# Fifteen small loads queued behind the first early store of a row-sum kernel

## The chip, the core and the metric

The kernel runs on one core of one Trainium2 chip. The metric is device time in microseconds (us), the median of several runs. The kernel before takes 161.08 us (median of 3 runs, 160.9 to 161.12).

## What is computed

```python
# x: float32 [32, 512, 1024]
relu_x = np.maximum(x, 0)
return np.sum(relu_x, axis=-1).astype(np.float32)     # float32 [32, 512]
```

The input is seen as 16,384 rows of 1,024 numbers, 64 MiB in all. Each row is clamped at zero and summed; the output is one number a row, 64 KiB.

## The kernel before

**Tiling.** Each of the 128 partitions holds 128 rows, counted as columns 0 to 127 of the tile `res` [128, 128], in which the sums gather. Rows come in blocks of 16 for each partition (8 MiB for a block) into three rotating tiles, `io0` to `io2`. There are seven full blocks and a tail of 16 rows, which is loaded in smaller and smaller pieces: 8 rows, 4 rows, then 2,302, 873 and 518 numbers of the last four rows, and at last 403 numbers into a small tile of its own, `last`.

**Work on a block.** ScalarE clamps a block or half a block in place (`clamp`, L145) and VectorE sums it (`total`, L153). In the last blocks and the tail both engines take single rows, with clamp and sum in one instruction: ScalarE in `act_row` (L160), VectorE in `dve_row` (L168); the parts of the last rows are `act_part` (L122) and `dve_part` (L127). GpSimd clamps one small piece (L246). A few matrix multiplies (L186) run near the end, whose product nobody reads. The last but one sum is finished by VectorE at L266, which reads `last` and so waits for the last load; the last one is finished by ScalarE with `act_part` on the rest of `last`.

**The SP queue.** SP (SyncE) issues all DMAs, in the order in which they are written. It issues the loads of the seven blocks (`load`, L104), of which those from the fourth on wait for VectorE to be done with the tile that they overwrite; then the six loads of the tail, of which the first waits; then three stores (`store`, L111 to L119):

- the early store of the first 16 columns of `res`, whose sums were done long before,
- the middle store of the next 110 columns, behind a wait at L115 for ScalarE and one on the DMA itself (L116) for VectorE,
- the last store of 2 columns, which waits for `sems.end`, that is for L266 and the last `act_part`.

Then SP clears the other semaphores (L51) and waits at L52 until all stores have landed: each DMA adds 16 to the semaphore `stored`, and `n_store` counts the DMAs that do so. With that the program ends. The order on each engine is written out by hand; no scheduler moves instructions. The first load stands ahead of everything else in the program.

Of the kernel before, what the change touches and what calls it, by code (L numbers as in the profile page):

```python
# [4 lines left out]
F32 = mybir.dt.float32  # L5
# [21 lines left out]

EARLY = 1
N_MM, MM_COLS = 8, 512


def kernel(tc: tile.TileContext, x: bass.AP, out: bass.AP):
    nc = tc.nc
    sems = Semaphores(tc)

    tc.close()
    tc.compile()
    nc.cur_bb = nc.bb_map[tc.start_bb_name]
    body = nc.cur_bb.bb.instructions
    ends = list(body)  # L40
    body.clear()
    n_stores = relu_sum(nc, sems, x, out)
    body.extend(ends)


    nc.cur_bb = nc.bb_map[tc.start_bb_name + "_end"]
    nc.cur_bb.bb.instructions.clear()
    nums = sorted(s.num for s in (*sems.loads, sems.act, sems.dve))
    cleared = range(nums[0], nums[-1] + 1)
    assert len(cleared) == len(nums)  # L50
    nc.sync.sem_clear(cleared)  # L51
    nc.sync.wait_ge(sems.stored, 16 * n_stores).then_inc(sems.stored, -16 * n_stores)  # L52
    open_without_barrier(tc, EARLY)
# [12 lines left out]
def relu_sum(nc, sems: Semaphores, x: bass.AP, out: bass.AP):  # L66
    x_flat = x.flatten_outer_dims()
# [27 lines left out]
    def sums(m, n):  # L95
        if m < ROWS:
            return of[:, m : m + n], res[:, m : m + n]
        return ov[:, m - ROWS : m - ROWS + n], res[:, m : m + n]
# [12 lines left out]
    def store(m, n, act, sem, count):  # L111
        nonlocal n_store
        dst, src = sums(m, n)
        if act:
            nc.sync.wait_ge(sems.act, act)  # L115
        nc.sync.dma_start(out=dst, in_=src).wait_op(sem, count, "sem-ge").then_inc(  # L116
            sems.stored, 16
        )
        n_store += 1  # L119
# [100 lines left out]
    for n in TAIL:  # L220
# [26 lines left out]
        out=clamped, in0=clamped, scalar1=0.0, scalar2=None, op0=MAX  # L247
    ).wait_op(loaded, 16, "sem-ge").then_inc(sems.end, 1)
    for lo, hi, n, first, second in (
# [9 lines left out]


    store(0, ROWS, freed[0][0], sems.dve, freed[0][1])
    store(ROWS, NT - ROWS - 2, sums_act, sems.dve, sums_dve)


# [2 lines left out]
        out=clamped,  # L267
# [59 lines left out]
```

## Time and profile before

| | |
|---|---|
| Median of 3 runs | 161.08 us (160.9 to 161.12) |
| Profiled execution, from its first to its last instruction (span) | 159.9 us; the page has no other time of it |
| Median less span | 1.2 us, around the span |
| VectorE busy | 118.7 us (74%) |
| ScalarE busy | 103.6 us (65%) |
| TensorE busy | 8.6 us (5%) |
| DMA packets of the kernel | 2304, 67.18 MB, 97.8% of 16 engines' time |
| Mean DMA rate over the span | 420 GB/s |
| Sixteen DMA issues of SP | 13 loads, 3 stores |

The profile is one execution on the chip. Times inside it count from the start of its span. "SPq" is the SP engine's queue of DMA issues; "idle before, releaser" names what ended a wait. The page's DMA share is the mean busy share of the 16 DMA engines that carry out what SP issues; a DMA over 128 partitions shows as 128 packets of data and 16 of 4 bytes, which are the increments of its semaphore: 16 DMAs with 144 packets each make the 2304. The trace also keeps the start, duration and size of every packet (without the number of its DMA engine), and the time at which each increment of a semaphore landed.

### The profile page before, as it was taken

To read this page: it belongs to the slowest core of one execution; us is meant where nothing else is said; L and a number is where in the kernel's file an instruction comes from. 1 tells how busy PE (TensorE), PEld (TensorE's weight loads), DVE (VectorE), ACT (ScalarE), POOL (GpSimd) and SP (SyncE) were. 2 spreads that over 40 slices of the span, in tenths; PEclk is the share of its full clock that TensorE was granted. 3 is DMA by queue.
4 is the path that set the end of the run, shared out by engine and by line. 5 is a ranking of instruction groups with operands and counts; after the bars stand their busy time and mean duration, and the time that the engine had idled before them with its cause. 6 is when DMAs were issued, how large, how long until landed. Compare 5 with 4: busy or idle time off the path is not lost.

```text
span 159.9 us, 157 instructions
## 1 busy us (share of the span) xinstructions
PE 8.6 (5%) x16; PEld 3.6 (2%) x16; DVE 118.7 (74%) x44; ACT 103.6 (65%) x53; POOL 1.0 (1%) x5
## 2 busy tenths in 40 slices
PE   0000000000000000000000000000000000000695
PEld 0000000000000000000000000000000000000241
DVE  0000000006999799999999999999999799999986
ACT  0000049993599807997099950999429993397995
POOL 0000000000000000000000000000000000000001
DMA  8996996996996997999979979969969969899993
GB/s 279 508 492 295 524 492 295 524 492 295 525 492 295 524 475 311 524 393 393 525 328 459 508 344 459 508 295 508 492 295 524 492 295 524 377 402 402 428 396 110
DMA packets 2304, 67.18 MB, mean 420 GB/s; under 512 B 640, under 2 KB 768, under 8 KB 1024
## 3 DMA queue, kind: packets, MB, share of 16 engines
q1 hardware_dynamic: 2304, 67.18, 97.8%
HBM read 67.11 MB, written 0.07 MB: 420 GB/s over the span
## 4 chain that ended last, share of the span: by engine, by line
DMA 45%; DVE 45%; ACT 9%; SPq 1%; issue 0%
DMA io<-in_x_dram 45%; DVE res L153 43%; ACT io L145 9%; DVE io L168 1%; SPq L104 1%; DVE io L127 1%; DVE io L266 0%
## 5 line engine op out<-in xcount | busy, mean ns | idle before, releaser
L153 DVE TENSOR_REDUCE res<-io 128x8 f32<-128x8192 f32 (+2 forms) x10 | 101.1, 10173 | 39.2 <-ACT io L145 39.2
L145 ACT ACTIVATE io<-io 128x8192 f32<-128x8192 f32 (+2 forms) x10 | 81.8, 8218 | 25.9 <-DMA io<-in_x_dram 25.9
L160 ACT ACTIVATE io<-io 128x1024 f32<-128x1024 f32 x18 | 18.8, 1042 | 6.6 <-DMA io<-in_x_dram 6.6
L186 PE MATMUL ps<-io 128*128 128x512 f32 x16 | 8.6, 698 | 149.5 <-DVE io L168 149.5
L168 DVE TENSOR_SCALAR_CACHE_REDUCE io<-io 128x1024 f32<-128x1024 f32 x14 | 16.2, 1215 | 0.5 <-DMA io<-in_x_dram 0.4
L143 ACT ACT_TABLE_LOAD x1 | 1.3, 1283 | 22.3 <-DMA io<-in_x_dram 22.3
L186 PEld LDWEIGHTS ps<-io 128*128 128x128 f32 x16 | 3.6, 231 | 153.7 <-DVE io L168 149.5
L160 ACT ACTIVATION_READ_ACCUMULATOR io<-io 128x1 f32 x18 | 3.3, 186 | 0.0
L246 POOL TENSOR_SCALAR io<-io 128x254 f32<-128x254 f32 x1 | 0.8, 841 | 155.4 <-DMA io<-in_x_dram 155.4
L168 DVE DVE_READ_ACCUMULATOR io<-io 128x1 f32 x14 | 1.2, 82 | 0.0
L127 DVE TENSOR_SCALAR_CACHE_REDUCE io<-io 128x552 f32<-128x552 f32 (+1 forms) x2 | 1.1, 594 | 0.0
L122 ACT ACTIVATE io<-io 128x321 f32<-128x321 f32 (+1 forms) x2 | 0.9, 426 | 0.1
L266 DVE SCALAR_TENSOR_TENSOR io<-last,io 128x254 f32<-128x254 f32 x1 | 0.4, 423 | 0.0
L122 ACT ACTIVATION_READ_ACCUMULATOR io<-io 128x1 f32 x2 | 0.4, 186 | 0.0
L122 ACT ACTIVATE last<-last 128x153 f32<-128x153 f32 x1 | 0.3, 330 | 0.0
L122 ACT ACTIVATION_READ_ACCUMULATOR last<-last 128x1 f32 x1 | 0.2, 187 | 0.0
L127 DVE DVE_READ_ACCUMULATOR io<-io 128x1 f32 x2 | 0.2, 82 | 0.0
L311 POOL MEMSET const-uint8-127<- 128x1 uint8 x1 | 0.1, 102 | 0.0
L311 POOL MEMSET const-bfloat16-1.0<- 128x1 bf16 x1 | 0.1, 101 | 0.0
L311 POOL MEMSET const-float32-0.0<- 128x1 f32 x1 | 0.1, 99 | 0.2 <-issue 0.2
L311 POOL MEMSET const-float32-1.0<- 128x1 f32 x1 | 0.1, 98 | 0.0
L266 DVE DVE_READ_ACCUMULATOR io<-last,io 128x1 f32 x1 | 0.1, 82 | 0.0
## 6 DMA issues: line engine op xcount, KB each, us to landing
io<-in_x_dram SPq DMA_DIRECT2D x1, 4096.0 KB, 23.7
io<-in_x_dram SPq DMA_DIRECT2D x1, 2048.0 KB, 28.3
io<-in_x_dram SPq DMA_DIRECT2D x1, 1151.0 KB, 30.6
io<-in_x_dram SPq DMA_DIRECT2D x1, 436.5 KB, 31.2
io<-in_x_dram SPq DMA_DIRECT2D x1, 259.0 KB, 31.4
last<-in_x_dram SPq DMA_DIRECT2D x1, 201.5 KB, 31.4
io<-in_x_dram SPq DMA_DIRECT2D x7, 29.0
out_dram<-res SPq DMA_DIRECT2D x1, 55.0 KB, 1.6
```

Source lines behind the costliest of these rows:

```text
L104: dma = nc.sync.dma_start(out=dst, in_=src)
L122: nc.scalar.activation(out=ap, in_=ap, func=RELU, accum_out=accum_out).wait_op(*after, "sem-ge").then_inc(sems.end, 1)
L127: i = nc.vector.tensor_scalar(out=ap, in0=ap, scalar1=0.0, scalar2=None, op0=MAX, op1=ADD, accum_out=accum_out,)
L143: nc.scalar.preload_act_table(RELU).wait_op(loaded, 16, "sem-ge")
L145: i = nc.scalar.activation(out=ap, in_=ap, func=RELU)
L153: nc.vector.tensor_reduce(out=res[:, m : m + n], in_=ap, axis=mybir.AxisListType.X, op=ADD).wait_op(sems.act, n_act, "sem-ge").then_inc(se ...
L160: i = nc.scalar.activation(out=ap, in_=ap, func=RELU, accum_out=accum_out)
L168: i = nc.vector.tensor_scalar(out=ap, in0=ap, scalar1=0.0, scalar2=None, op0=MAX, op1=ADD, accum_out=accum_out,)
L186: i = nc.tensor.matmul(ps[:, :], rows_of[:, 0, :P], rows_of[:, 1, :MM_COLS], start=True, stop=True)
L246: nc.gpsimd.tensor_scalar(out=clamped, in0=clamped, scalar1=0.0, scalar2=None, op0=MAX).wait_op(loaded, 16, "sem-ge").then_inc(sems.end, 1)
L266: nc.vector.scalar_tensor_tensor(out=clamped, in0=last[:, : 2 + LAST_DVE], scalar=0.0, in1=clamped, op0=MAX, op1=ADD, accum_out=res[:, NT ...
L311: nc = _bacc.Bacc("TRN2", target_bir_lowering=False, num_devices=1)
```

## The change

Fifteen loads are put between the early store and the middle store. Load n, for n from 1 to 15, takes the first 20 + n numbers (84 to 140 bytes) of the first n rows of x, into a new tile `probe` of 16 partitions; no instruction reads that tile. The new loads wait for nothing, are issued from SP like the others, and add to `stored`, so that L52 waits for them too (18 DMAs instead of 3). No other instruction changes; from L29 on lines are numbered one higher, and eight higher from L262 on.

```diff
@@ -27,6 +27,7 @@
 
 EARLY = 1
 N_MM, MM_COLS = 8, 512
+PROBES, PROBE_COLS = 15, 64
 
 
 def tile_relu_sum_kernel(tc: tile.TileContext, x: bass.AP, out: bass.AP):
@@ -259,6 +260,13 @@
 
 
     store(0, ROWS, freed[0][0], sems.dve, freed[0][1])
+    probe = nc.alloc_sbuf_tensor("probe", [16, PROBES * PROBE_COLS], F32)
+    for n in range(1, PROBES + 1):
+        to = (n - 1) * PROBE_COLS
+        nc.sync.dma_start(
+            out=probe[:n, to : to + 20 + n], in_=x_flat[:n, : 20 + n]
+        ).then_inc(sems.stored, 16)
+        n_store += 1
     store(ROWS, NT - ROWS - 2, sums_act, sems.dve, sums_dve)
 
 
```

## The prediction

> **What bounds the kernel now.** I read the chain that ended last first, as shares and then its last pieces in order of time, since the change touches only the end of the DMA-issuing queue (SP).
>
> ```profile
> DMA io<-in_x_dram 45%; DVE res L153 43%; ACT io L145 9%; DVE io L168 1%; SPq L104 1%; DVE io L127 1%; DVE io L266 0%
> ```
>
> ```profile
> 125.15 30.57 DMA io<-in_x_dram
> 155.72 0.02 issue
> 155.75 1.23 DVE io L168 x2
> 156.97 1.05 DVE io L127 x4
> 158.03 0.02 issue
> 158.05 0.43 DVE io L266 x2
> ```
>
> The input stream (67 MB) sets the time almost to the end. From 125.15 us on the chain is the tail's loads; then short VectorE pieces, and L266, which needs two things: the DVE parts before it (done at 158.01) and the last load. The trace's landing records put the sixteen increments of that load at 157.10 to 158.03, fourteen of them by 157.56 and the other two at 157.91 and 158.03. So the tail is a tie of VectorE and the last load, and whatever delays that load delays the end one for one.
>
> Next the SP queue's timeline from 124 us on, and its waits:
>
> ```profile
> 124.29 2.31 SPq L104 DMA_DIRECT2D io<-in_x_dram  x5
> 126.65 0.44 SPq L104 DMA_DIRECT2D last<-in_x_dram  x1
> 127.21 31.63 SPq L116 DMA_DIRECT2D out_dram<-res  x3
> ```
>
> ```profile
> SPq L104 <- DVE res L153: 121.6, 5, 53.3
> SPq L115 <- ACT io L160: 29.3, 1, 29.3
> SPq L116 <- DVE io L266: 1.1, 1, 1.1
> SPq L52 <- SPq L52: 1.0, 1, 1.0
> ```
>
> Every load of the tail is issued by 127.1. The early store (rows 0 to 15) is issued at 127.21 and takes 0.38; then SP waits 29.3 us at L115, till 156.92, issues the middle store at 157.00, and the last store at 158.51. The DMA issues and the DMA share of the last microseconds:
>
> ```profile
> out_dram<-res SPq DMA_DIRECT2D x1, 55.0 KB, 1.6
> out_dram<-res SPq DMA_DIRECT2D x1, 8.0 KB, 31.0
> out_dram<-res SPq DMA_DIRECT2D x1, 1.0 KB, 1.4
> ```
>
> ```profile
> 156.00:157.00 1.00, 1.00 (x3) 0.38 (x2) 1.00 (x3) 1.00 (x3) 0.64 (x1) 1.00 0.95 333
> 157.00:158.00 1.00, 1.00 (x3) 0.19 (x1) 1.00 (x4) 0.90 (x4) 0.00 (x0) 1.00 0.22 60
> 158.00:159.00 1.00, 0.10 (x1) 0.00 (x0) 0.44 (x4) 0.43 (x3) 0.00 (x0) 1.00 0.09 23
> 159.00:160.00 1.00, 0.00 (x0) 0.00 (x0) 0.00 (x0) 0.00 (x0) 0.00 (x0) 1.00 0.08 1
> ```
>
> The early store took 31.0 us to land because each DMA engine works its queue in order: the packet records have none of its 64-byte packets before 156.55, after the last load's packets on that engine. So the fifteen new loads, queued behind it, run there too, after 156.5. And there (the last but one column) the DMA engines are busy 22%, 9% and 8% of the time.
>
> **The change part by part.** Nothing is removed. All is made against the profiled execution's 159.9 us; the median of the timed runs, 161.08, stands 1.2 above, and I carry that over.
>
> *SP's time.* Fifteen issues. The sixteen issues of this trace took 0.33 to 0.49 us each, so 5.0 to 7.3 us. SP reaches L115 at 132.6 to 134.9 instead of 127.6 and waits there 22 to 24 us instead of 29.3. Price 0. The new loads wait for no semaphore, and behind them are only the two stores and L52. The cover is gone when one issue costs over 29.3 / 15 = 1.95 us, four times the dearest row; beyond that each microsecond delays the middle store, and the last store once 1.5 more are used.
>
> *The loads ahead.* All thirteen loads of x are issued before the new ones, and engines take packets in order, so no packet of x goes later. Price 0; the bound upward is one engine's whole new work (next step).
>
> *DMA engines.* The new loads make 1 + 2 + ... + 15 = 120 rows of 84 to 140 bytes, 13 KB. A packet's time in the records: 1612 bytes 68 ns, 2072 bytes 85 ns, thus 0.037 ns a byte and 8.4 ns fixed; the small ends are 64 bytes 11 ns and 4 bytes (a completion) 9 ns. So a new packet is about 12 to 14 ns with 9 for its completion. If each partition goes to its own engine, the first engine gets fifteen: 15 x 22 = 0.33 us. If every row went to one engine: 120 x 13 + 15 x 9 = 1.7 us. On the latest engine the early store's packets end at 157.64, the middle store's fill 157.84 to 158.18, and the last store's start at 159.34. Idle there: 0.20 + 1.16 = 1.36 us; on most engines 0.5 to 0.9 more. 0.33 fits; 1.7 would stick out by 0.3 on the latest engine alone. I take 0.33, hence price 0: the middle store goes perhaps 0.13 later, and only L52 at 159.9 wants it.
>
> *Completions.* What the trace doesn't show is a row of fifteen tiny DMAs, each closing with a completion. The nearest row is the early store behind the last load: on the earliest engine they landed at 157.10 and 157.29, on the latest at 158.03 and 158.20, so 0.17 to 0.19 apart, though 0.065 of packets lay between. So one more DMA in an engine's queue costs from its packets, 0.02, to 0.17 or so if a completion must be acknowledged before the next DMA's data is written. 15 x 0.02 = 0.3, hidden as above; 15 x 0.17 = 2.6, not hidden (rival 1). I take the lower, because the 0.17 includes the early store's eight packets and a write to HBM, where the new loads write one packet to SBUF. Nothing in this makes the kernel faster: no wait is shortened, and below nothing I allow only the scatter of the runs.
>
> That fixed costs of DMAs overlap, the landings show: the last three loads landed at 156.85, 157.51 and 158.03, 0.66 and 0.52 apart, as their bytes need, while one store alone takes 1.4 us from issue to landing. The Trainium skill (DMA: Bandwidth & Descriptors, "Anatomy of one DMA") has about 2 us fixed for each DMA, most of it the write receipt, and calls the bubble of the semaphore write itself tiny. Paid one after another that would be an estimated 30 us here; by the landings just given the trace agrees with the tiny bubble and not with the sum.
>
> *The end.* L52 now waits for 18 landings instead of 3. The new ones land by about 158.5 (157.7 to 158.2 for the early store, plus 0.3), the last store at 159.91. Price 0. Sum: 159.9 + 0 = 159.9, and with 1.2 outside the span 161.1.
>
> **The rivals.**
>
> 1. *Completions in single file.* Each new load holds its engine's queue 0.17 us. The first engine has all fifteen: from 157.3 to 157.7, where the early store landed on the fourteen earlier engines, 2.6 us lead to 159.9 to 160.3; the middle and the last store land 0.17 each behind: 160.2 to 160.6, or 161.1 if this engine is the latest one (158.20). That is 0.3 to 1.2 over 159.9: 161.4 to 162.3, most likely 161.7. It decides from (159.9 - 157.7 - 0.34) / 15 = 0.12 us each on a normal engine. For it: the 0.17 of the early store. Against it: the reason given above.
> 2. *Small writes are slow.* A load below some size makes its engine read the place and write it back, so twice the 0.17: 15 x 0.34 = 5.1, from 157.5 to 162.6, the stores to 162.9: 3.0 more, 164.1. Against it: the 64-byte and 8-byte packets of the stores run at 11 and 9 ns, but those write to HBM. The Trainium skill (DMA: Bandwidth & Descriptors, "Specifications") says that transfers under 512 bytes are done as read-modify-write, which speaks against this change; the stores' rows show no such price.
> 3. *SP stalls on too many DMAs in flight.* At 127.6 eight DMAs were unfinished and SP was not held; now up to 23 are. With a limit of eight, each new load waits for a landing: the eighth goes out at 158.2, seven more and two stores at 0.45 each end at 162.3, and 1.4 to land: 163.7, 3.8 more: 164.9. For it: nothing above eight is seen. Against it: 0.38 for the eighth, no longer than the first load's 0.38.
> 4. *The last load lands later.* New packets on the earlier engines disturb the two late ones. At most one engine's 0.33 goes on the path: 161.4.
> 5. *The loads don't go out as written* (merged, or one row to many packets): packets come to other than 2304 + 120 + 120 to 240 completions; with the windows above still 161.1, so it shares the forecast's time.
>
> **How the numbers follow.** No change, at 160.8 to 161.4: 0.55 (rival 5 in it). Rival 1: 0.20. Rival 4: 0.08. Rival 3: 0.06. Rival 2: 0.04. Faster for a reason that I don't see: 0.07. The runs before spread over 160.9 to 161.12, so 0.2% (0.32 us) is about what can be told from no change. Slower: 0.20 + 0.08 + 0.06 + 0.04 = 0.38; same 0.55; faster 0.07. The range 160.8 to 162.0 holds the first case, rival 4 and most of rival 1, together 0.8; rivals 2 and 3, the upper end of rival 1 and a real gain are left out.
>
> **What would show it.** Right: fifteen issues of 0.33 to 0.5 us from 127.6 on, the wait at L116 (L115 before) 22 to 24 us and ended by ScalarE, the new packets after 156.5, L274 (L266 before) starting at 158.05 and the last store landing 1.4 us after its issue. Rival 1 and 2: that landing takes 1.7 to 4.4 us, with the chain's end the same. Rival 3: the wait at L116 gone and the middle store issued after 158. Rival 4: the last load's increments after 158.03. A stall of SP during the 128 to 156 us, or any new load's packet before 156, would make the whole reading wrong.

## The result

The changed kernel takes 162.24 us (median of 4 runs, 161.94 to 162.26) against 161.1 us of the kernel before, run beside it: a ratio of 1.0067, with a 95% interval of 1.0055 to 1.0079. So fifteen loads with 13 KB of data, which nobody reads, cost 1.1 us. The forecast was no change at 161.1 us, in a range of 160.8 to 162.0; the measured time lies outside it.

### The profile page after: what moved, and what is told of

Its sections match the earlier page's. It is cut to its first block, busy times and chain, and to the rows that moved or that the text cites. A ratio compares the mean times of both kernels' runs of the same rounds, so it can differ in the third digit from the quotient of the medians.

```text
span 160.9 us, 172 instructions
## 1 busy us (share of the span) xinstructions
PE 10.0 (6%) x16; PEld 4.0 (3%) x16; DVE 118.8 (74%) x44; ACT 103.6 (64%) x53; POOL 1.0 (1%) x5
## 2 busy tenths in 40 slices
DMA packets 2544, 67.19 MB, mean 418 GB/s; under 512 B 880, under 2 KB 1008, under 8 KB 1264
## 3 DMA queue, kind: packets, MB, share of 16 engines
q1 hardware_dynamic: 2544, 67.19, 97.5%
## 4 chain that ended last, share of the span: by engine, by line
DMA 43%; DVE 36%; ACT 12%; PE 6%; SPq 0%; issue 0%
DMA io<-in_x_dram 43%; DVE res L154 31%; ACT io L146 12%; PE ps L187 6%; DVE io L169 6%; SPq L105 0%
## 5 line engine op out<-in xcount | busy, mean ns | idle before, releaser
L187 PE MATMUL ps<-io 128*128 128x512 f32 x16 | 10.0, 798 | 149.3 <-DVE io L169 149.3
L128 DVE TENSOR_SCALAR_CACHE_REDUCE io<-io 128x552 f32<-128x552 f32 (+1 forms) x2 | 1.1, 596 | 0.0
L128 DVE DVE_READ_ACCUMULATOR io<-io 128x1 f32 x2 | 0.2, 82 | 0.0
```

The lines of the kernel that those rows point to most:

```text
L128: i = nc.vector.tensor_scalar(out=ap, in0=ap, scalar1=0.0, scalar2=None, op0=MAX, op1=ADD, accum_out=accum_out,)
L187: i = nc.tensor.matmul(ps[:, :], rows_of[:, 0, :P], rows_of[:, 1, :MM_COLS], start=True, stop=True)
```

## The profile after

The chain of the changed kernel, first as shares, then its last pieces in order of time (start, duration, what):

```profile
DMA io<-in_x_dram 43%; DVE res L154 31%; ACT io L146 12%; PE ps L187 6%; DVE io L169 6%; SPq L105 0%
```

```profile
124.95 15.15 DVE res L154 x2
140.09 9.12 DVE io L169 x16
149.22 0.04 issue
149.26 10.04 PE ps L187 x16
```

This chain misleads, and it is worth seeing why. It is followed back from the last instruction that an engine other than SP carried out, and that happens to be a matrix multiply, at 159.3 us, whose product nobody reads. The program ends at 160.9, when SP's last wait ends; the chain doesn't start there. The compute that the last store waits for did not end later than before. VectorE's last sum, which needs the last load (start, duration, instruction):

```profile
157.84 0.42 DVE L274 SCALAR_TENSOR_TENSOR io<-last,io 128x254 f32<-128x254 f32 x1
158.19 0.08 DVE L274 DVE_READ_ACCUMULATOR io<-last,io 128x1 f32 x1
```

That is 0.2 us earlier than the 158.05 of before. The last load wasn't late. So the time was lost after the computing was over. The SP queue's timeline from the tail's loads on, and its waits:

```profile
126.38 0.44 SPq L105 DMA_DIRECT2D last<-in_x_dram  x1
126.94 0.40 SPq L117 DMA_DIRECT2D out_dram<-res  x1
127.39 24.06 SPq L266 DMA_DIRECT2D probe<-in_x_dram  x15
156.76 1.91 SPq L117 DMA_DIRECT2D out_dram<-res  x2
```

```profile
SPq L105 <- DVE res L154: 121.3, 5, 53.1
SPq L116 <- ACT io L161: 5.2, 1, 5.2
SPq L53 <- SPq L53: 2.1, 1, 2.1
SPq L117 <- DVE io L274: 1.2, 1, 1.2
```

Two lines changed. The wait for the landings at the end, L53, is 2.1 us where L52 had 1.0: this is the loss. And the fifteen issues took 24.06 us, not 5 to 7, so that the wait for ScalarE shrank from 29.3 to 5.2 us. The line of these issues gives the shortest, median and longest in ns:

```profile
L266 SPq DMA_DIRECT2D probe<-in_x_dram x15: 344/1172/4677, 127.4 to 150.8; - x15
```

The last microseconds by windows (the last but one column is the DMA engines' busy share):

```profile
156.00:157.00 1.00, 1.00 (x4) 0.38 (x3) 1.00 (x3) 1.00 (x3) 0.40 (x1) 1.00 1.04 373
157.00:158.00 1.00, 1.00 (x4) 0.52 (x3) 0.94 (x5) 0.83 (x5) 0.00 (x0) 1.00 0.56 101
158.00:159.00 1.00, 1.00 (x4) 0.24 (x2) 0.27 (x2) 0.26 (x2) 0.00 (x0) 1.00 0.00 0
159.00:160.00 1.00, 0.31 (x1) 0.00 (x0) 0.00 (x0) 0.00 (x0) 0.00 (x0) 1.00 0.08 1
160.00:161.00 1.00, 0.00 (x0) 0.00 (x0) 0.00 (x0) 0.00 (x0) 0.00 (x0) 1.00 0.00 0
```

By this column the DMA engines are idle from 158 on, but for 8%, while SP waits 2.1 us for them. Every one of the 120 new data packets had started by 157.4 and the last store's packets by 159.35, each 7 to 14 ns long. What comes late is not shown as packets: it is the landings. The trace's records of the increments of `stored` end like this (us):

```
159.99 160.00 160.06 160.14 160.15 160.16 160.18 160.19 160.33 160.34 160.36 160.37
160.51 160.53 160.70 160.71 160.88
```

They come as a staircase of 0.17 to 0.19 us, fewer on each step, and the last is alone at 160.88. Before, the sixteen increments of the last store all came within 0.17 us, at 159.74 to 159.91. There are 183 increments in all: 48 of the three stores; 15 that come 0.13 to 0.18 us after the end of an issue of a new load, long before any of its packets ran, and so are taken to be SP's own; and 120, one for every partition of a new load. From these counts load n is taken to have run on n engines, one packet and one completion on each, so that one engine, called the first here, has all fifteen. The packet records have no engine number that would show it directly.

## Theories

A completion is the increment of the semaphore that a DMA leaves on each engine that it uses. Theory A: on each DMA engine completions land in single file, 0.18 us apart, whatever the DMA carries. An engine with c completions behind the last load lands the last of them at about 157.6 + 0.18 c inside the span; with 15 new ones and three stores, c = 18 and this is 160.84. The last store lands anyhow at about 159.8, so below c = 12 nothing is seen. B: all 120 packets or completions count together, on whatever engine they are. C: small writes are dear, those under the 512 bytes of rival 2 of the prediction. D: loads on fewer than sixteen engines are dear. F: each load waits for its own read of HBM.

## Experiments

Unless the diff says otherwise, an edit is made to the changed kernel. Times before were 161.01 to 161.05 us in these comparisons.

### One row for each load

```diff
-            out=probe[:n, to : to + 20 + n], in_=x_flat[:n, : 20 + n]
+            out=probe[:1, to : to + 35], in_=x_flat[:1, :35]
```

> Fifteen loads as in the change, but each of one row of 140 bytes, so 15 packets and 15 completions in all instead of 120 and 120. Theory A (on each DMA engine the completions of its queue land in single file, 0.18 us apart, whatever they carry; the first engine has the early store, fifteen new loads, the middle and the last store, 18 in all, from 157.6 us): the same first engine, so the same time as the changed kernel, 162.2 us, span 160.9, last landings 0.18 apart. Rival B (all 120 packets or completions count together, for instance at the semaphore that they share): an eighth of the cost, 161.2 us.

Measured: 162.01 us (ratio 1.0061, 1.0048 to 1.0073). An eighth of the packets and completions, and nearly the whole cost. The last increments come at 160.09, 160.28, 160.46 and 160.64, one at a time. B falls: what counts is the fullest engine. SP was held as in the change (the second issue 4.2 us, then 2.4), so one engine with many packets queued is enough for that too.

### One load with all the packets

```diff
-    for n in range(1, PROBES + 1):
...
+    nc.sync.dma_start(
+        out=probe[:16, :, :35],
+        in_=x_flat[: 16 * PROBES, :35].rearrange("(p r) c -> p r c", p=16),
+    ).then_inc(sems.stored, 16)
```

> One load in place of the fifteen: 16 partitions with 15 pieces of 140 bytes each, so 15 small packets on every engine, more bytes than the change has (34 KB), but one completion on each engine. Theory A (completions in single file): one completion more, 0.18 us, hidden: 161.1 us. Rival C (each write under 512 bytes is dear, by reading and writing back): every engine has as many small writes as the first one of the change, 162.2 us or more. If the issue is held up by a full queue, SP is held here as well, as 16 descriptors stand against the 30 of the change.

Measured: 161.29 us (ratio 1.0017, 1.0008 to 1.0026). Fifteen small packets on every engine in one load cost 0.28 us, against 1.1 us for fifteen loads; C falls for packets of 140 bytes. The 0.28 was not expected by A, and it is no completion: L53 waits 1.0 us as before. VectorE's last sum started at 158.11, 0.27 later than in the change, 0.03 after the last load's last increment (158.08); before it VectorE was idle for 0.17 us. The bracket names L128, VectorE's own piece, but that had ended at 157.93:

```profile
158.11 0.42 DVE L273 SCALAR_TENSOR_TENSOR io<-last,io 128x254 f32<-128x254 f32 x1 [0.17 <-DVE io L128]
```

That increment came 0.64 us behind that of the load ahead of it, against 0.54 in the change and 0.52 before. So about 0.1 us is a delay of the last load itself, which is rival 4 of the prediction in small. The rest was there with the load ahead already (157.44 against 157.28 in the change) and isn't explained. SP's issue took 0.68 us, without a hold-up; that tells little, since nothing was queued behind it until 156.7 us.

### Seven loads and eleven

```diff
-PROBES, PROBE_COLS = 15, 64
+PROBES, PROBE_COLS = 7, 64
```

> Only the loads of 1 to 7 partitions. Theory A: the first engine has 7 + 3 completions, 157.6 + 10 x 0.18 = 159.4, before the last store could land anyway (159.7 to 159.9): 161.1 us, no change, a threshold at 8 or 9 loads. A rival in which each load costs the same on the path (1.1 / 15 = 0.075 us) gives 161.6 us.

Measured with seven: 161.08 us (ratio 1.0003, 0.9994 to 1.0012): no cost, with a span of 159.8 us. SP was held for 16.8 us all the same, so the hold-up itself costs nothing here.

```profile
127.40 16.80 SPq L266 DMA_DIRECT2D probe<-in_x_dram  x7
156.79 1.88 SPq L117 DMA_DIRECT2D out_dram<-res  x2
```

With `PROBES` at 11:

> Only the loads of 1 to 11 partitions. Theory A: 14 completions on the first engine, 157.6 + 14 x 0.18 = 160.1 inside the span against 159.8 to 159.9 without: 161.3 to 161.5 us, between seven loads (161.1, nothing) and fifteen (162.2). In proportion to the loads: 161.9.

Measured: 161.44 us (ratio 1.0024, 1.0013 to 1.0034), with the last increment at 160.19. A threshold and then a slope, as A has it; a price in proportion to the loads is ruled out by both.

### Rows of 640 bytes

```diff
-PROBES, PROBE_COLS = 15, 64
+PROBES, PROBE_COLS = 15, 160
...
-            out=probe[:n, to : to + 20 + n], in_=x_flat[:n, : 20 + n]
+            out=probe[:n, to : to + 160], in_=x_flat[:n, :160]
```

> The fifteen loads of 1 to 15 partitions with 640 bytes a row instead of 84 to 140. Theory A: the same fifteen completions on the first engine, packets of 32 ns by the line through the load packets are shorter than the 0.18 between completions: 162.2 us, as the change. Rival C (writes under 512 bytes are dear): the cost is gone, 161.1 to 161.3 us.

Measured: 162.52 us (ratio 1.0090, 1.0076 to 1.0103). With 640 bytes the cost is not gone, so C falls altogether; the steps stay 0.18 (160.80, 160.98, 161.16). The 0.3 us on top of the change show at the start of the single file: 161.16 less 18 x 0.18 is 157.92, against 157.64 in the change. That fits the last load, which the file stands behind: its last increment came 0.86 us behind that of the load before it. VectorE waited for it too, but the program's end isn't its:

```profile
158.12 0.42 DVE L274 SCALAR_TENSOR_TENSOR io<-last,io 128x254 f32<-128x254 f32 x1 [0.38 <-DVE io L128]
```

### Sixteen partitions for each load

```diff
-            out=probe[:n, to : to + 20 + n], in_=x_flat[:n, : 20 + n]
+            out=probe[:16, to : to + 35], in_=x_flat[:16, :35]
```

> Fifteen loads of 16 partitions with 140 bytes each, so that every DMA engine gets fifteen packets and fifteen completions. Theory A (completions in single file on each engine): the time of the change, 162.2 us, or up to 0.3 more, as the two late engines now have eighteen completions behind the last load too (157.8 to 158.0 + 18 x 0.18 = 161.0 to 161.3 inside the span). Rival D (only loads on fewer than sixteen engines are dear, as SP itself adds the rest of the sixteen increments): no cost, 161.1 us, and issues of 0.4 us without the hold-up of 2.4 us. If a full queue holds SP, the issues last as long as in the change.

Measured: 162.72 us (ratio 1.0108, 1.0091 to 1.0125), with the last increment at 161.32; a little above what A gave. All sixteen engines have fifteen new completions now (288 increments, none of them SP's), the late ones too. D falls, for the cost and for the hold-up, which is the same:

```profile
L266 SPq DMA_DIRECT2D probe<-in_x_dram x15: 443/1172/4853, 127.2 to 150.9; - x15
```

### Thirty loads

```diff
-PROBES, PROBE_COLS = 15, 64
+PROBES, PROBE_COLS = 30, 64
...
-            out=probe[:n, to : to + 20 + n], in_=x_flat[:n, : 20 + n]
+            out=probe[:1, to : to + 35], in_=x_flat[:1, :35]
```

> Thirty loads of one row of 140 bytes. Theory A: 33 completions in single file on the first engine, 157.6 + 33 x 0.185 = 163.7 us inside the span, 164.9 us in all. A cost in proportion to the loads, without a threshold, gives 163.3 (161.1 + 2 x 1.1). SP, held up in every issue, reaches its wait at 156.7 us only after it was over, so the middle store goes out late, at some 159 us, but this is hidden behind the single file.

Measured: 164.73 us (ratio 1.0231, 1.0215 to 1.0246), with the last increment at 163.35. Against fifteen loads of one row, 163.35 - 160.64 = 2.71 us for fifteen more completions: 0.181 each. The part on SP was wrong: the last fourteen issues took only 0.25 to 0.27 us, and SP still came to its wait before it was over, with 0.7 us to spare:

```profile
127.43 28.63 SPq L266 DMA_DIRECT2D probe<-in_x_dram  x30
```

```profile
SPq L53 <- SPq L53: 4.6, 1, 4.6
SPq L117 <- DVE io L274: 1.1, 1, 1.1
SPq L116 <- ACT io L161: 0.7, 1, 0.7
```

### The loads ahead of the stream

```diff
     for j in range(NB):
+        if j == NBUF:
+            probe = nc.alloc_sbuf_tensor("probe", [16, PROBES * PROBE_COLS], F32)
+            for n in range(1, PROBES + 1):
...
-    probe = nc.alloc_sbuf_tensor("probe", [16, PROBES * PROBE_COLS], F32)
-    for n in range(1, PROBES + 1):
...
```

> The same fifteen loads, but issued right after the third load of x, when SP waits some 53 us for VectorE. They stand in the engines' queues at about 61 us, ahead of the fourth to seventh load. Theory A in its weak form (only completions wait for each other, data behind them flows on): nothing is left at the end, 161.1 us. In its strong form (the writes of the data behind them wait too): the first engine is held up 15 x 0.18 = 2.7 us once, and as the stream of loads has no gap after that, up to 2.7 us stay: up to 163.8 us.

Measured: 162.98 us (ratio 1.0125, 1.0096 to 1.0154). Less is hidden here: dearer than at the end. The four runs differ more than elsewhere (162.56 to 163.55), and the profile is that of the longest. The increments of the fourth load, the first behind the fifteen, came at 79.84 to 82.50, where in the change they came at 79.40 to 80.02. So its latest engine is 2.48 us later; fifteen steps of 0.18 are 2.7. On one engine, by these times that one, the small packets went on until 62.70, and only then its first 64 KB packet began; the other fifteen engines began theirs at 59.80 to 60.49. The delay is never made up: the last load's increments end at 160.25 instead of 157.82. So the strong form of A holds for the engine that ends last, whose data waited. It doesn't hold step by step: engines with one load fewer after another should make an even staircase, but the last two increments are 81.50 and 82.50. Nor did packets wait in the change, where all small ones had run by 157.41 and the last store's by 159.35, while completions landed until 160.88. How many packets may run ahead of the completions is not shown.

SP's issues were not held up at all here:

```profile
0.00 1.33 SPq L105 DMA_DIRECT2D io<-in_x_dram  x3
1.37 5.44 SPq L200 DMA_DIRECT2D probe<-in_x_dram  x15
```

Eighteen DMAs were unfinished then, but on the first engine at most 3 x 9 + 15 x 2 = 57 packets. In the change SP is held when the second new load is issued, with ten unfinished, but by this count some 70 packets on the first engine: some 5 of the seventh block's 9, 54 of the tail's six loads, 9 of the early store and 2 of the first new load.

### Copies in SBUF and stores to HBM

```diff
-            out=probe[:n, to : to + 20 + n], in_=x_flat[:n, : 20 + n]
+            out=probe[:n, to : to + ROWS], in_=res[:n, :ROWS]
```

> The fifteen loads become copies inside SBUF: 64 bytes a row from the first columns of res into the new tile, 1 to 15 partitions, the same place in the queue. Tells what the 0.18 us are. If they are the acknowledgement of the write to SBUF (theory A), the steps stay 0.18 and the time 162.2 us. If each transfer waits for its own read of HBM (rival F), the steps shrink, and at under 0.12 the time is back at 161.1 us.

Measured: 162.18 us (ratio 1.0078, 1.0061 to 1.0095), the last increments in steps of 0.18 to 0.19 (160.02, 160.21, 160.40, 160.57). F falls: no read of HBM is in it. (Its 197 increments say that the copy of one row was spread over all sixteen engines; the first engine has fifteen copies as before.) The same edit, with `probe` in HBM:

> The fifteen become stores of 64 bytes a row from res to a scratch tensor in HBM. If the step between completions is the acknowledgement of a write, it may be another one here: the early store landed 0.17 to 0.19 us behind the last load, of which 0.06 is its packets. With steps of 0.18 the time is 162.2 us, with 0.12 it is 161.2, and with 0.25 it is 163.2 (157.6 + 15 x 0.25 + 0.5 = 161.9 inside the span).

Measured: 162.01 us (ratio 1.0066, 1.0051 to 1.0081), steps of 0.18 (160.10, 160.27, 160.45, 160.63). Where the data goes makes no difference to the step, and none to the time that is clear of the noise.

### The last store on a queue of its own

```diff
-    store(NT - 2, 2, 0, sems.end, 16 + 6 + 2)
+    dst, part = sums(NT - 2, 2)
+    nc.scalar.dma_start(out=dst, in_=part).wait_op(
+        sems.end, 16 + 6 + 2, "sem-ge"
+    ).then_inc(sems.final, 16)
...
+    nc.sync.wait_ge(sems.final, 16).then_inc(sems.final, -16)
     nc.sync.sem_clear(cleared)
```

> The change, but the last store is issued by ScalarE, on a DMA queue of its own, with a semaphore of its own; the fifteen loads and the other stores stay with SP. If the single file is one for each engine and queue, the last store lands 1.4 us after its issue, at about 159.9, and the program ends with the middle store behind the fifteen, 157.6 + 17 x 0.18 = 160.7 inside the span: 161.9 to 162.0 us. If the file is one for each engine, across the queues, the last increments of the last store come at 160.7 to 160.9, and the time is that of the change, 162.2 us.

Measured: 162.47 us (ratio 1.0092, 1.0077 to 1.0107). The last store's packets began at 159.08 on the second queue, but its increments end at 160.53 and 160.72, the last of them 0.18 behind the last of the first queue's (160.54). The file is one for each engine, across queues. The last store's semaphore is its own here, so a semaphore that all share is not the cause either. By the Trainium skill (DMA: Bandwidth & Descriptors, "Queues, rings and completion order") the semaphore write lands only after every earlier write of that engine, across its queues; the trace agrees. The 0.2 us over the change are the edit's own: SP now clears its semaphores between the two last waits, and ends at 160.91 with what it had at 160.73.

## Why the prediction was wrong

All runs with the loads behind the early store: completions behind the last load on the fullest engine (c), the time that 157.6 + 0.18 c gives, and the last increment in the profile. The 157.6 was fitted to the change; the single file starts behind the last load, and so moves with it by some tenths between runs.

| run | c | 157.6 + 0.18 c | last increment |
|---|---|---|---|
| one load with all the packets | 4 | 158.3 (hidden) | 159.96 |
| seven loads | 10 | 159.4 (hidden) | 159.73 |
| eleven loads | 14 | 160.1 | 160.19 |
| the change | 18 | 160.8 | 160.88 |
| one row each | 18 | 160.8 | 160.64 |
| rows of 640 bytes | 18 | 160.8 | 161.16 |
| sixteen partitions each | 18 | 160.8 | 161.32 |
| copies in SBUF | 18 | 160.8 | 160.57 |
| stores to HBM | 18 | 160.8 | 160.63 |
| last store on its own queue | 18 | 160.8 | 160.72 |
| thirty loads | 33 | 163.5 | 163.35 |

- **The step that failed is "Completions".** It had the right bounds, 0.02 to 0.17 us for one more DMA in a queue, and the right consequence at the upper end, and took the lower end. The measured value is 0.18. The nearest row, the early store 0.17 to 0.19 behind the last load, had been the price itself; I explained it away by its eight packets and its write to HBM. The runs with other packets, sizes and targets show that none of these matters to the step.
- **The argument from the last loads was the wrong one.** That they landed 0.66 and 0.52 apart shows only that the wait is hidden where a DMA carries 0.5 us of data on each engine. It says nothing of DMAs whose data take 0.013 us. The tiny bubble of the semaphore write in the Trainium skill (DMA: Bandwidth & Descriptors, "Anatomy of one DMA"), which I had read as agreeing, agrees at most with the packet records (9 ns). That section tells of DMAs issued by GpSimd, and these are SP's. Between the completions of small DMAs there were 0.18 us in every run that had a row of them.
- **Rival 1 is what happened.** The last store landed 2.6 us after its issue (158.30 to 160.88), where the prediction gave 1.7 to 4.4 for rivals 1 and 2, and 1.4 if it was right. Rival 1 gave 161.4 to 162.3, most likely 161.7, at a chance of 0.20. The likeliest value was low since the step is 0.18 and not 0.17 (0.2 us over 17 of them) and because the early store lands on the first engine at about 157.8 by the formula, not 157.5. The rival had the engine's queue held; in the change only the landings were, as all the new packets had run by 157.41. The range ended at 162.0, inside this rival's own span; with that chance the range should have held the whole of it.
- **SP's time was mis-sized, at no price.** 24.06 us for fifteen issues instead of 5.0 to 7.3, most likely because the queue of the first engine was full. The rows of the trace had no issue with that many packets queued. The cover of 29.3 us held, as the seven loads show, but with 5.2 us left instead of 22. Rival 3 had a hold-up in mind that goes by the number of DMAs; the early placement, with eighteen and no hold-up, speaks against that. The prediction had named a stall of SP between 128 and 156 us as a sign that the whole reading is wrong. The stall came, but it isn't what failed.
- **DMA engines, loads ahead, compute: right.** The packets took 12 to 14 ns, as worked out, all after 156.8; the last load's increments ended at 157.82, not later than before; VectorE's last sum did not start later. Rival 4 came true only with more bytes, and in part: behind the load ahead of it the last load landed 0.1 us later with 34 KB in one load, and 0.3 with 77 KB. Rival 2 is out. Rival 5 too: there are 2544 packets, and with one completion for each partition this is 2304 + 120 + 120.

What stays open: what happens in the 0.18 us (it holds for reads of HBM and of SBUF, and for writes to both), when data waits with the completions, and how many packets fill an engine's queue; the runs put it between 57 and about 70, by counting, and no run was made for it alone.

## What to carry to other kernels

Count DMAs, not bytes, on the fullest DMA engine: each small one cost 0.18 us there in these runs, the landing of all that is queued behind it waits, and the transfer that the program ends on should not stand behind more of them than the compute tail covers (here about eight by the formula; seven cost nothing, eleven 0.4 us). Merge small transfers into one DMA: one load of 240 pieces cost a quarter of fifteen loads of 120. When the chain ends on an engine that nobody waits for, read the queue's last wait and the landings instead.

## What was not expected of the hardware

- Small DMAs can hold up the data stream behind them: with the fifteen ahead of the fourth load its last engine landed 2.48 us later than in the change, and 1.9 us of the time (medians) were lost by it.
- An issue on SP lasted 0.24 to 0.68 us where it wasn't held, and up to 4.85 us where, by the count above, one engine's queue was full. In the change the second new issue lasted 4.68 us, the next five 2.4 and the others 1.2 or 0.6. The last three times are about what the stream's packets take: 2.418 (64 KB), 1.213 (32 KB) and 0.611 us (16 KB). The match is not one to one: three of the issues of 2.4 us ended after 137.75, when the 64 KB packets were over.
- The DMA engines' busy share is 0 in a microsecond (158 to 159 us) in which completions hold up the end of the program: waiting for a completion is not counted as busy.
